# Moving the right-hand SBUF pools of a transformer trunk 32 bytes further in

## The chip, the cores and the metric

The kernel runs on one core of a Trainium2 chip. The metric is the device time of one execution in microseconds. The program before the change took 2705.5, 2704.69 and 2701.03 us in three runs; the median is 2704.69 us. All data is float32, and there is one launch.

## The reference, cut to what matters

Two layers over 1024 tokens of width 1024. The first mixes the tokens with a forgetting attention of 16 heads, the second with a gated MLP whose gate is mixed over blocks of 128 tokens; behind each comes a gated MLP ("FFN") with a short causal convolution.

```
for i in range(2):
    h = modulate(rmsnorm(x, norm1_g[i]), sh1, sc1)
    y = forgetting_attention(h, ...)  if i == 0  else  spatial_gating_mlp(h, ...)
    x = x + g1 * y
    h = modulate(rmsnorm(x, norm2_g[i]), sh2, sc2)
    x = x + g2 * conv_gated_ffn(h, w_up[i], conv_w[i], conv_b[i], w_down[i])
return rmsnorm(x, final_g)
```

The up-projections are `h @ w_up` (1024 x 1024 by 1024 x 5632, twice) and `h @ sgu_w_in` (1024 x 1024 by 1024 x 4096). The vectors `sh`, `sc`, `g` come from six matrix-vector products per layer ("ada") of the conditioning vector `c` after SiLU.

## The kernel before, in words

**Products.** Every float32 product is made of three: each operand is held as a rounded high part and a low rest, and `mm3` (L107) issues high x high, high x low and low x high into one PSUM bank. Each of these is one weight load of the stationary operand (128 x 128) and one matmul that streams the moving operand (mostly 128 x 512).

**Stages.** The attention stage (`fox`) runs to about 827 us of the trace. Then FFN 0, the gated MLP (SGU) and FFN 1 follow. Each of these three has an up part (`up`, L1333) and a down part (`down`, L1468).

**The up part.** A unit is one pair of 128-column slices of the weight. There are 22 units in each FFN and 16 in the SGU. The first two units of a stage are done plainly: eight products of 12 matmuls each (`half1`, `half2`). All later units, 20 + 14 + 20 = 54 of them, are done in seven products (Strassen's scheme in Winograd's form): `p1`, `p5`, `p6`, `p2`, `p7`, `p3`, `p4`, in that order. Each calls `seven` (L1278), which issues 4 x 3 = 12 matmuls into one PSUM bank. The moving operands are seven prepared combinations of the activations, named B11, T1, T2, B21, T3, B22 and T4 in the order of the products; they lie in fourteen tiles `hc0` to `hc13`, two to an operand, and stay for the whole stage. The stationary operands are combinations of the weights, made afresh for every unit in a ring of four tiles `ow0` to `ow3`: a load into `rw` by DMA, sums on VectorE (`sums_u`), and the split into high part (ScalarE, L1131) and low part (VectorE, L1144).

`p1` and `p2` (B11, B21) go to one bank, called `banka` in FFN 0 and FFN 1; `p5` and `p3` (T1, B22) to `bankY`; `p6`, `p7`, `p4` (T2, T3, T4) to `bankX`. After every down part the names `a` and `X` are swapped (L1613), so in the SGU B11 and B21 go to `bankX` and T2, T3, T4 to `banka`.

**The down part.** Both operands of a matmul lie in one `ow` tile: the stationary one in its first half, the moving one in its second.

**Where the tiles lie.** A pool opened without a side grows from the low end of each SBUF partition, a pool with `side="right"` from the high end. The allocator rounds every tile up to 32 bytes. Adding up the tiles in the order of their pools gives their first bytes:

- left: `const`, `small`, `tm`, `x`, `h`, `qkv`, and from the FFN on `hc13` and `hc0` to `hc8`. `hc13` starts at byte 43968, `hc8` at 117696. `x` starts at 11200, and the last `h` tile at 105408. `x`, `h`, `qkv` and these `hc` tiles all start on a multiple of 64.
- right, below byte 229344, which is 32 above a multiple of 64: in the attention `cv`, `raw`, `w` (32 above a multiple of 64), `qq`, `kh`, `kl`, `pt` (a multiple of 64); from the FFN on `hc9` to `hc12` (`hc9` at 135136), `rw`, `ow` (`ow0` at 184288) and `pp0` to `pp2`, all 32 above a multiple of 64.

The parts of a tile that a matmul reads begin at multiples of 512 bytes within these tiles. So with a stationary operand in `ow`, the moving operands B11 and B21 (`hc9` to `hc12`) lie on the same remainder modulo 64 as the weights, and T1, T2, T3, T4 and B22 (`hc13`, `hc0` to `hc8`) lie on another.

**Order of the work.** In the up and down parts TensorE's instructions are chained in program order (`strict`, L103). What TensorE waits for there is an `ow` tile, and so VectorE and ScalarE and, behind them, the DMA into `rw`, all issued on SyncE's queue in program order. `cact` (SiLU of `c`) is read by VectorE in the ada products (L266), and `qg` by ScalarE and VectorE (L695, L697).

Of the kernel before, what the change touches and what calls it, by code (L numbers as in the profile page):

```python
# [8 lines left out]
F32 = mybir.dt.float32  # L9
# [9 lines left out]
P = 128  # L19
S = 1024  # L20
D = 1024
KT = D // P
# [45 lines left out]
class Trunk:  # L68
# [96 lines left out]
    def setup(self):  # L165
        nc, tc, ctx = self.nc, self.tc, self.ctx
        en = ctx.enter_context
        self.const = en(tc.tile_pool(name="const", bufs=1))
        self.small = en(tc.tile_pool(name="small", bufs=3))
        self.tm = en(tc.tile_pool(name="tm", bufs=2))  # L170
        self.xp = en(tc.tile_pool(name="xp", bufs=1, reuse_waits="tile"))
        self.ms = en(tc.tile_pool(name="ms", bufs=2, space=PSUM))
        self.dram = en(tc.tile_pool(name="dram", bufs=1, space=DRAM))
        c = self.const
        self.ident = c.tile([P, P], F32, name="ident")
        make_identity(nc, self.ident)
        self.ones = c.tile([P, P], F32, name="ones")
        nc.vector.memset(self.ones, 1.0)

        self.prm = c.tile([P, 5 * P + 2 * KT], F32, name="prm")  # L180
        self.at = {}
        kp = lambda a: a.rearrange("(k p) -> k p", p=P)
        self.cact = c.tile([P, KT], F32, name="cact")
        first = self.tile(self.tm, [P, 512], F32, "tm")[: 2 * KT, :P]
        o = 5 * P
        for e, nm, src, n in (
            (nc.sync, "c", self.c[0], KT),
            (nc.scalar, "n1_0", self.norm1_g[0], KT),
        ):
            e.dma_start(first[o - 5 * P : o - 5 * P + n], kp(src))  # L190
            self.at[nm] = o
            o += n
        ps = self.tile(self.ms, [P, 512], F32, "ms")
        self.chain("ms", nc.tensor.transpose(ps[:, 0 : 2 * KT], first, self.ident[: 2 * KT, : 2 * KT]))
        nc.vector.tensor_copy(self.prm[:, 5 * P :], ps[:, 0 : 2 * KT])
        self.chain("act", nc.scalar.activation(self.cact, self.col("c", 0, KT), AF.Silu))
        self.mod = {}

        adab = self.tile(self.tm, [P, 512], F32, "tm")[:48, :256]
        self.adabt = c.tile([P, 48, 2], F32, name="adabt")  # L200
        nc.scalar.dma_start(adab, self.ada_b.rearrange("l (r f) -> (l r) f", f=256))
        ps = self.tile(self.ms, [P, 512], F32, "ms")
        for j in range(2):
            i = nc.tensor.transpose(
                ps[:, j * 48 : j * 48 + 48], adab[:, j * P : (j + 1) * P], self.ident[:48, :48]
            )
            if j == 0:
                self.chain("ms", i)
        nc.vector.tensor_copy(self.adabt, ps[:, :96].rearrange("p (j r) -> p r j", j=2))
# [135 lines left out]
    def fox(self):  # L345
        nc, tc = self.nc, self.tc
        w_in, w_out = self.fox_w_in[0], self.fox_w_out[0]
        en = self.ctx.enter_context
# [5 lines left out]
        c = self.const  # L354

        with ExitStack() as es:
# [9 lines left out]
            def T(shape, dt, tag, bufs):  # L366
                return (mp if tag in ("qkv", "fraw") else fp).tile(shape, dt, tag=tag, name=self.name(tag), bufs=bufs)
# [9 lines left out]
            def ps1(nm):  # L377
                return ps_f.tile([P, 512], F32, tag="ps", name=self.name(nm))
# [143 lines left out]
                    o_out(p, half, ps[half])  # L522


            qg = T([P, 1], F32, "qg8", 1)
            nc.vector.tensor_scalar(qg, self.col("qg", 0), DH ** -0.5, None, op0=ALU.mult)
            kg = self.col("kg", 0)
            bf = T([P, H], F32, "bf", 1)
# [509 lines left out]
            for m in range(KT):  # L1038
# [5 lines left out]
                ps = open_ps.get(m) or (banks() if banks else ps1("op"))  # L1044
# [884 lines left out]
```

## Time and profile before

| | |
|---|---|
| median of three runs | 2704.69 us |
| the profiled execution | 2712.99 us |
| its span, first to last instruction | 2711.2 us |
| mean granted TensorE clock | 0.978 |
| TensorE matmuls busy | 2597.6 us, 96% |
| VectorE busy | 2082.7 us, 77% |
| ScalarE busy | 1462.7 us, 54% |
| attention | 0 to 827 us |
| FFN 0: up part, down part | 827 to 1284, 1284 to 1498 us |
| SGU: up part, down part | 1498 to 1870, 1870 to 2030 us |
| FFN 1: up part, down part | 2030 to 2479, 2479 to 2711 us |

The chain of waits is the work that ended last, followed back from the last instruction; a row gives its start and its length in us, the engine, the tile it writes and its line, and how many instructions were merged. A row of the grouped instructions gives the line, engine, operation, tiles (written <- read), shapes and count, then busy us and mean ns of one, then the idle time ahead of it with what ended it. Matmuls overlap, so the mean duration of one is longer than the step from one start to the next; the chain of waits goes by that step.

### The profile page before, as it was taken

To read this page: it belongs to the slowest core of one execution; us is meant where nothing else is said; L and a number is where in the kernel's file an instruction comes from. 1 tells how busy PE (TensorE), PEld (TensorE's weight loads), DVE (VectorE), ACT (ScalarE), POOL (GpSimd) and SP (SyncE) were. 2 spreads that over 40 slices of the span, in tenths; PEclk is the share of its full clock that TensorE was granted. 3 is DMA by queue.
4 is the path that set the end of the run, shared out by engine and by line. 5 is a ranking of instruction groups with operands and counts; after the bars stand their busy time and mean duration, and the time that the engine had idled before them with its cause. 6 is when DMAs were issued, how large, how long until landed. Compare 5 with 4: busy or idle time off the path is not lost.

```text
span 2711.2 us, 35378 instructions
## 1 busy us (share of the span) xinstructions
PE 2597.6 (96%) x12578; PEld 2190.2 (81%) x12578; DVE 2082.7 (77%) x3609; ACT 1462.7 (54%) x2321; POOL 170.4 (6%) x289
## 2 busy tenths in 40 slices
PE   6999999998999999999999999999998999999997
PEld 5988888898777788788888788888876888888886
DVE  7678777888567888888678866765888788877875
ACT  7347666777555445445446544654465545455444
POOL 1122222222200000000000000000000000000000
PEclk9999999998999999999999999999999999999999
DMA  7751111113232344546645346557552343337462
GB/s 230 242 173 53 55 53 53 55 52 109 77 115 70 124 130 135 177 136 204 242 156 172 108 154 185 183 177 271 160 179 73 97 136 115 114 101 280 159 202 90
DMA packets 316521, 379.46 MB, mean 140 GB/s; under 512 B 18872, under 2 KB 196152, under 8 KB 316344
## 3 DMA queue, kind: packets, MB, share of 16 engines
q1 hardware_dynamic: 316120, 377.14, 42.8%
q8 instruction: 99, 1.62, 0.2%
q14 instruction: 78, 0.64, 0.1%
q10 hardware_dynamic: 224, 0.06, 0.0%
HBM read 287.41 MB, written 89.72 MB: 139 GB/s over the span
## 4 chain that ended last, share of the span: by engine, by line
PE 80%; DVE 10%; ACT 4%; DMA 3%; issue 2%; SPq 0%; POOL 0%; DVEq 0%; ACTq 0%; POOLq 0%
PE bankX L104 20%; PE banka L104 18%; PE bankY L104 18%; PE pj L104 7%; PE ms L104 4%; PE o L104 3%; PE s L104 2%; PE ms L157 2%; PE op L104 2%; PE pv L104 2%; DVE ow L1144 1%; DVE hc L1144 1%; PE ms L1753 1%; DVE x L1144 1%; DVE x L1632 1%
## 5 line engine op out<-in xcount | busy, mean ns | idle before, releaser
L1131 ACT CAST ow<-rw 128x1024 fp32r<-128x1024 f32 (+1 forms) x438 | 398.1, 910 | 480.2 <-PE bankY L104 160.8
L1144 DVE TENSOR_TENSOR ow<-rw,ow 128x1024 fp32r<-128x1024 f32 (+1 forms) x438 | 457.6, 1046 | 182.0 <-ACT ow L1131 181.3
L104 PE MATMUL bankX<-hc,ow 128*128 128x512 f32 x1920 | 480.7, 399 | 17.8 <-DVE ow L1144 10.0
L104 PEld LDWEIGHTS bankX<-hc,ow 128*128 128x128 f32 x1920 | 361.5, 190 | 104.4 <-DVE ow L1144 11.9
L104 PE MATMUL banka<-hc,ow 128*128 128x512 f32 x1608 | 396.2, 395 | 1.1 <-DVE ow L1144 1.1
L104 PE MATMUL bankY<-hc,ow 128*128 128x512 f32 x1584 | 396.7, 398 | 0.0
L104 PEld LDWEIGHTS banka<-hc,ow 128*128 128x128 f32 x1608 | 301.4, 189 | 67.7 <-DVE ow L1144 1.4
L104 PEld LDWEIGHTS bankY<-hc,ow 128*128 128x128 f32 x1584 | 296.8, 188 | 70.6 <-issue 1.9
L104 PE MATMUL pj<-x,h 128*128 128x384 f32 (+1 forms) x1536 | 317.3, 349 | 0.2 <-DVE x L119 0.2
L104 PEld LDWEIGHTS pj<-x,h 128*128 128x128 f32 x1536 | 273.1, 194 | 5.0 <-DVE x L119 0.5
L1632 DVE SCALAR_TENSOR_TENSOR x<-x,prm,x 128x1023 f32<-128x1023 f32 (+1 forms) x160 | 204.4, 1279 | 2.7 <-ACT x L1630 2.1
L104 PE MATMUL bankY<-ow 128*128 128x512 f32 x720 | 203.8, 391 | 0.2 <-DVE x L1148 0.2
L104 PE MATMUL banka<-ow 128*128 128x512 f32 x672 | 187.4, 392 | 0.5 <-DVE x L1148 0.5
L104 PEld LDWEIGHTS bankY<-ow 128*128 128x128 f32 x720 | 135.4, 189 | 28.5 <-DVE x L1148 0.6
L104 PE MATMUL bankX<-ow 128*128 128x512 f32 x588 | 156.6, 393 | 0.2 <-DVE ow L1144 0.2
L104 PEld LDWEIGHTS banka<-ow 128*128 128x128 f32 x672 | 125.9, 188 | 27.2 <-ACT x L1181 0.8
L104 PE MATMUL ms<-ow 128*128 128x512 f32 x546 | 140.0, 391 | 0.9 <-DVE pp L1144 0.9
L104 PE MATMUL pv<-pt,w 128*128 128x256 f32 (+1 forms) x640 | 119.1, 296 | 16.2 <-ACT pt L795 13.0
L119 DVE TENSOR_TENSOR pt<-ms,pt 128x512 fp32r<-128x512 f32 (+1 forms) x160 | 100.2, 632 | 41.6 <-ACT pt L795 39.8
L104 PEld LDWEIGHTS bankX<-ow 128*128 128x128 f32 x588 | 110.9, 189 | 24.2 <-issue 0.8
L104 PEld LDWEIGHTS ms<-ow 128*128 128x128 f32 x546 | 102.1, 188 | 23.7 <-DVE pp L1144 2.9
L795 ACT CAST pt<-ms 128x512 fp32r<-128x512 f32 (+1 forms) x160 | 85.2, 539 | 64.7 <-PE ms L157 55.1
(302 smaller groups left out, 3886.2 us busy)
## 6 DMA issues: line engine op xcount, KB each, us to landing
rw<-yd SPq DMA_DIRECT2D x210, 256.0 KB
rw<-in_ffn_w_up_dram SPq DMA_DIRECT2D x88, 512.0 KB
yd<-pp SPq DMA_DIRECT2D x60, 512.0 KB
rw<-in_ada_w_dram SPq DMA_DIRECT2D x48, 512.0 KB
rw<-in_ffn_w_down_dram SPq DMA_DIRECT2D x88, 256.0 KB
rw<-in_sgu_w_in_dram SPq DMA_DIRECT2D x32, 512.0 KB
yd<-x SPq DMA_DIRECT2D x30, 512.0 KB
fraw<-in_fox_w_in_dram SPq DMA_DIRECT2D x96, 128.0 KB
```

Source lines behind the costliest of these rows:

```text
L104: i = self.nc.tensor.matmul(out, lhsT, rhs, start=start, stop=stop, skip_group_check=self.strict)
L119: return (eng or self.nc.vector).tensor_tensor(lo, full, hi.bitcast(F32), op=ALU.subtract)
L157: i = self.nc.tensor.transpose(ps[: s.shape[1], j * P : (j + 1) * P], s, self.ident)
L795: nc.scalar.copy(pt[:, 0, :nb], ps[:, :nb])
L1131: return self.ao(self.nc.scalar.copy(t[:, 0], src))
L1144: return self.vo(self.nc.vector.tensor_tensor(out, a, b, op=op))
L1632: stt(o[:, j:], a[:, : S - j], w[2 - j], o[:, j:], op0=ALU.mult, op1=ALU.add)
L1753: k = nc.tensor.matmul(px[:, b * P : (b + 1) * P], vn[:, b, c * P : (c + 1) * P], sg[:, 0], start=True, stop=True)
```

## The change

A new pool `rim` is opened on the right side, ahead of the other right-hand pools, and `cact` moves into it. It holds 8 float32 numbers per partition, 32 bytes, so all other right-hand tiles come to lie 32 bytes lower. `prm` on the left grows by 8 columns (32 bytes, unused), in the place that `cact` leaves, so all left-hand tiles stay where they are; the copy into `prm` names its columns outright. `qg` takes 9 columns, of which one is used, so its place in the pool grows from 32 to 64 bytes: the tiles of that pool that lie below it (`qq`, `kh`, `kl`, `pt` among them) move by 64 bytes in all and keep their remainder. No instruction is added or taken away.

```diff
+        self.rim = en(tc.tile_pool(name="rim", bufs=1, side="right"))
...
-        self.prm = c.tile([P, 5 * P + 2 * KT], F32, name="prm")
+        self.prm = c.tile([P, 5 * P + 3 * KT], F32, name="prm")
...
-        self.cact = c.tile([P, KT], F32, name="cact")
+        self.cact = self.rim.tile([P, KT], F32, name="cact")
...
-        nc.vector.tensor_copy(self.prm[:, 5 * P :], ps[:, 0 : 2 * KT])
+        nc.vector.tensor_copy(self.prm[:, 5 * P : 5 * P + 2 * KT], ps[:, 0 : 2 * KT])
...
-            qg = T([P, 1], F32, "qg8", 1)
+            qg = T([P, KT + 1], F32, "qg8", 1)[:, :1]
```

## The prediction

> **What bounds the kernel.** I read the page first, then the chain of waits stage by stage, then the groups of instructions.
>
> ```profile
> span 2711.2 us, 35378 instructions
> PE 2597.6 (96%) x12578; PEld 2190.2 (81%) x12578; DVE 2082.7 (77%) x3609; ACT 1462.7 (54%) x2321; POOL 170.4 (6%) x289
> ...
> PE 80%; DVE 10%; ACT 4%; DMA 3%; issue 2%; SPq 0%; POOL 0%; DVEq 0%; ACTq 0%; POOLq 0%
> ```
>
> TensorE is the bound: 80% of the chain that ended last is its own matmuls. So the step from one matmul to the next sets the time. Here is one whole seven-product unit of FFN 0 in the chain, with no other work in between:
>
> ```profile
> 1262.37 2.80 PE bankX L104 x12
> 1265.17 2.72 PE banka L104 x12
> 1267.89 2.80 PE bankY L104 x12
> 1270.70 2.80 PE bankX L104 x12
> 1273.50 2.75 PE banka L104 x12
> 1276.24 2.80 PE bankX L104 x12
> 1279.04 2.80 PE bankY L104 x12
> 1281.84 2.33 PE bankX L104 x10
> ```
>
> Same shapes, same count, no wait, yet two rates. The two banka blocks (B11, B21) take 2.72 and 2.75 us; the five others (T4, T1, T2, T3, B22) take 2.80. The unit takes 1281.84 - 1262.37 = 19.47 us.
>
> Is it the bank? In the SGU the names are swapped, and the fast rate goes with the operand (bankX is now B11 and B21):
>
> ```profile
> 1801.59 2.72 PE bankX L104 x12
> 1804.31 2.80 PE bankY L104 x12
> ...
> 2049.32 2.72 PE banka L104 x12
> 2052.04 2.72 PE bankY L104 x12
> 2054.76 2.80 PE bankX L104 x12
> ```
>
> The last three rows are the plain first units of FFN 1: bankY holds 2.72 while it takes B21, and the next block, the first with T1, is back at 2.80. So neither bank nor scheme decides, but the moving operand's tile.
>
> Two more places tell what about the tile. In the down part both operands lie in one right-hand tile; in the attention's first projections both lie on the left:
>
> ```profile
> 1330.00 0.68 PE banka L104 x3
> ...
> 1344.96 0.68 PE bankX L104 x3
> ...
> 119.98 18.17 PE o L104 x80
> ```
>
> From 1330.00 to 1344.96 there are 22 such rows, 66 matmuls in 14.96 us: 226.7 ns each, or 2.72 us for twelve. On the left it is 18.17/80 = 227.1 ns. The slow blocks take 2.80/12 = 233.3 ns. Right with right (remainders 32 and 32) is fast, left with left (0 and 0) is fast, left with right (0 and 32) is slow.
>
> **The change, part by part.** It adds 32 bytes to the offset between left and right and leaves every left-left and right-right pair as far apart as before, but for the attention's small pool. Exactly the slow blocks are touched. No instruction, wait or DMA is added or moved past a queue.
>
> *The seven-product units.* All 84 matmuls at 226.7 ns make 84 x 0.2267 = 19.04 us instead of 19.47: 0.43 us a unit. With 54 units: 23.2 us. This takes for granted that the 2.75 blocks too come down to 2.72; they start behind a slow block, and the 2.72 blocks of FFN 1 above start behind a fast one.
>
> The Trainium skill speaks against this. "TensorE: Matmul & The Clock Gate", Part 2, first step of the step-by-step, says that TensorE has two independent read ports into SBUF and that loading the next weights takes no bandwidth from the matmul that runs. By that rule it cannot matter where the two operands begin, and the time would stay at 2704.69 us. The trace does not agree: 2.80 against 2.72 us for twelve equal matmuls.
>
> *What of it is not on the chain.* PE's gain counts only where PE sets the end. In FFN 0 the chain leaves it once in mid-stage:
>
> ```profile
> 1087.34 2.80 PE bankX L104 x12
> ...
> 1115.39 6.69 DMA rw<-in_ada_w_dram
> ...
> 1130.51 1.15 DVE ow L1144
> ...
> 1131.70 2.60 PE bankX L104 x10
> ```
>
> From about 1087 to 1131.70, 44 us, it runs over DMAs and VectorE, and what PE gains there is lost: 2.2 units at 20 us, -0.9 us. At the head of each stage the chain runs over VectorE, which makes the seven operands:
>
> ```profile
> 882.00 1.20 DVE hc L1144 x2
> ...
> 888.58 4.63 PE bankX L104 x10
> ...
> 1555.62 1.14 DVE ow L1144
> ...
> 1556.80 2.60 PE banka L104 x10
> ```
>
> The slow blocks of the first two units (8 a stage, 0.08 us each) and some of the third lie ahead of these points. I count them at nothing and take 0.3 us off for the third unit. If all counted it would be +24 x 0.08 = 1.9 us.
>
> *The attention.* There the mixed pairs are `pv` (pt 0, w 32) and the transposes (ident 0; cv, raw, w 32), against equal ones with `x`, `qkv` and `s`:
>
> ```profile
> L104 PE MATMUL pv<-pt,w 128*128 128x256 f32 x512 | 107.8, 306 | 16.2 <-ACT pt L795 13.0 <-DVE pt L119 3.2
> L104 PE MATMUL s<-kh,qq 128*128 128x256 f32 x32 | 9.6, 313 | 0.0
> L157 PE MATMUL ms<-ident,x 128*128 128x128 f32 x152 | 22.4, 272 | 0.0
> L157 PE MATMUL ms<-ident,w 128*128 128x128 f32 x16 | 3.2, 274 | 0.0
> ```
>
> 306 against 313 ns and 274 against 272: no loss to win back, so 0. The bound: 640 `pv` matmuls by the 6.7 ns of the wide ones, 4.3 us.
>
> *VectorE, ScalarE, DMA.* Their operands change remainder too. VectorE's mixed and equal pairs of today cost the same (688 and 691 ns):
>
> ```profile
> L1144 DVE TENSOR_TENSOR rw<-rw,rw 128x512 f32<-128x512 f32 x108 | 74.3, 688 | 1.5
> L1144 DVE TENSOR_TENSOR hc<-hc,rw 128x512 f32<-128x512 f32 x30 | 20.7, 691 | 9.9 <-DMA rw<-in_ffn_w_down_dram 6.6 <-DMA rw<-in_sgu_w_out_dram 3.1
> ```
>
> So 0, and 0 for ScalarE, whose copies read one tile. For landings the trace gives no pair to compare. DMA has 3% of the chain (81 us), and the slow blocks are 3% longer than the fast ones (2.80 to 2.72); 3% of 81 either way is 2.4 us, an estimate for the range. `cact` is read at its new place by the same instructions: 0.
>
> **Sum.** 23.2 - 0.9 - 0.3 = 22.0 us. Against the profiled execution of 2712.99 us (span 2711.2 and 1.8 around it) that gives 2691; it lies 8.3 us above the median of the runs, so against the median 2704.69 - 22.0, rounded to 2682 us.
>
> **The rivals.** *Only a part of it comes (2692 us).* Left-hand moving operands might reach 2.75 us and not 2.72, as blocks do that today follow a slow one. The unit is then 7 x 2.75 = 19.25, 0.22 us less, 12 us in all with the same losses taken in. For it: B11 and B21 stand at 2.75 in nearly every unit. Against: 18.17/80 on the left.
>
> *Left and right differ by themselves (2704 us).* If it is the distance or the side, and not the remainder, a shift of 32 bytes does nothing. The rule of the Trainium skill above ends at the same time. For it: no fast pair in the trace has one operand on each side. Against: `hc8` lies 184288 - 117696 = 66592 bytes below `ow0` and is slow (B22, the row at 1279.04), while `hc9` lies 49152 below it and is fast, in the row at 1265.17 (B11); and left-hand pairs lie up to 94208 bytes apart (`h` to 105408, `x` from 11200) at 227.1 ns. That the change doesn't do what it says, because some tile's size upsets the remainders, ends here too; adding up the sizes, I find none that does.
>
> *Slower: VectorE becomes the bound, and the clock falls.* The place is the up part of the FFNs:
>
> ```profile
> 900.00:1100.00 200.00, 200.00 (x875) 162.23 (x873) 172.01 (x201) 100.66 (x123) 0.00 (x0) 1.00 0.40 129
> ...
> 883.00:894.00 11.00, 6.42 (x15) 4.59 (x16) 10.96 (x12) 2.19 (x4) 0.00 (x0) 0.53 0.23 72
> ...
> 888.58 4.63 PE L104 MATMUL bankX<-hc,ow 128*128 128x512 f32 x10 [4.45 <-DVE ow L1144]
> 893.01 3.22 PE L104 MATMUL banka<-hc,ow 128*128 128x512 f32 x12
> ```
>
> VectorE is busy 172.01 of 200 us (86%). Where PE waited 4.45 us for it, the granted clock over the next 11 us was 0.53, and ten matmuls took 4.63 us instead of 2.27: 2.4 us lost. Nine such stretches eat the gain; from there it is slower, and one in every second unit of the FFNs (20) gives 20 x 2.4 - 22 = +26, 2731 us. Against: a faster unit raises VectorE's share to 86% x 19.47/19.04 = 88%, still short of full, and PE stood still for none of those 200 us.
>
> **How the numbers follow.** The forecast 0.82, the part 0.06, no effect 0.08, slower 0.04. The range runs from all bounds at once (23.2 + 1.9 + 4.3 + 2.4 is 31.8, 2673) to the partial gain (2692); the two other rivals are left out. A time within 0.2% (5.4 us) cannot be told from no change; the first two cases are faster, the third the same.
>
> **What would show it.** In the changed profile the bankX and bankY blocks of twelve in the up parts should stand at 2.72 us like those of the down parts, and the mean of the `hc,ow` groups near that of the `ow` ones:
>
> ```profile
> L104 PE MATMUL bankX<-hc,ow 128*128 128x512 f32 x1920 | 480.7, 399 | 17.8 <-DVE ow L1144 10.0
> ...
> L104 PE MATMUL bankY<-ow 128*128 128x512 f32 x720 | 203.8, 391 | 0.2 <-DVE x L1148 0.2
> ```
>
> FFN 0 should shrink by about 7.7 us, the SGU by 6, FFN 1 by 8.5, the attention and the down parts by nothing. Blocks still at 2.80 would prove the remainder wrong; blocks at 2.72 with longer waits for `ow` would prove that PE was not the bound.

## The result and the profile after

The changed kernel took 2688.12 us (median of five runs) against 2703.49 us of the kernel before in the same series: a ratio of 0.9938 with a 95% interval of 0.9919 to 0.9956, some 17 us less. A second series gave 2685.14 against 2705.7 us, a ratio of 0.992 (0.9907 to 0.9934), some 22 us less. The ratios are taken over all runs of a series; the medians alone are 15.4 and 20.6 us apart. The forecast was 2682 us in a range of 2673 to 2692, 22.0 us less.

The page of the changed kernel (line numbers are two higher below the change):

```profile
span 2686.3 us, 35378 instructions
PE 2573.0 (96%) x12578; PEld 2186.3 (81%) x12578; DVE 2078.6 (77%) x3609; ACT 1463.1 (54%) x2321; POOL 171.5 (6%) x289
...
PE 78%; DVE 11%; ACT 4%; DMA 3%; issue 2%; SPq 1%; POOL 0%; DVEq 0%; ACTq 0%; POOLq 0%
```

TensorE's busy time fell by 2597.6 - 2573.0 = 24.6 us, no other engine's by more than 4.1. The last unit of FFN 0 in the chain of waits of the changed kernel (start, length, what):

```profile
1254.26 2.72 PE banka L104 x12
1256.98 2.72 PE bankY L104 x12
1259.70 2.72 PE bankX L104 x12
1262.42 2.72 PE banka L104 x12
1265.14 2.72 PE bankX L104 x12
1267.86 2.72 PE bankY L104 x12
1270.58 2.72 PE bankX L104 x12
1273.30 0.45 PE ms L104 x2
```

All seven blocks stand at 2.72 us, and the unit takes 1273.30 - 1254.26 = 19.04 us, to the hundredth what the forecast had. At the head of FFN 1, in the same view, the block that was the first slow one now follows at the same step:

```profile
2034.50 2.72 PE bankY L104 x12
2037.22 2.72 PE bankX L104 x12
```

The groups of matmuls (busy us, mean ns of one, idle time ahead) with the moving operand in `hc` come down to those of the down part:

```profile
L104 PE MATMUL bankX<-hc,ow 128*128 128x512 f32 x1920 | 471.3, 394 | 18.5 <-DVE ow L1146 10.3 <-ACT ow L1133 7.8 <-DVE x L1146 0.3
...
L104 PE MATMUL bankY<-hc,ow 128*128 128x512 f32 x1584 | 387.9, 391 | 0.8 <-DVE ow L1146 0.8
...
L104 PE MATMUL bankY<-ow 128*128 128x512 f32 x720 | 203.3, 390 | 0.2 <-DVE x L1150 0.2
```

By stages, from the first `hc` matmul of an up part to its last, in two profiles of each kernel:

| | before | before, again | after | after, again |
|---|---|---|---|---|
| attention and lead-in, us | 827.4 | 819.6 | 823.9 | 825.0 |
| up part of FFN 0 | 456.9 | 456.9 | 449.0 | 449.4 |
| up part of the SGU | 371.5 | 371.6 | 365.9 | 367.2 |
| up part of FFN 1 | 448.7 | 450.0 | 441.3 | 440.0 |
| the three up parts | 1277.0 | 1278.5 | 1256.2 | 1256.6 |
| the profiled execution | 2712.99 | 2707.06 | 2688.12 | 2688.01 |

The up parts lost 20.8 us in the first pair and 22.0 in the second.

### The profile page after: what moved, and what is told of

Same layout as the page of the kernel before. It is cut to its first block, busy times and chain, and to the rows that moved or that the text cites. A ratio compares the mean times of both kernels' runs of the same rounds, so it can differ in the third digit from the quotient of the medians.

```text
span 2686.3 us, 35378 instructions
## 1 busy us (share of the span) xinstructions
PE 2573.0 (96%) x12578; PEld 2186.3 (81%) x12578; DVE 2078.6 (77%) x3609; ACT 1463.1 (54%) x2321; POOL 171.5 (6%) x289
## 3 DMA queue, kind: packets, MB, share of 16 engines
q1 hardware_dynamic: 316120, 377.14, 43.5%
## 4 chain that ended last, share of the span: by engine, by line
PE 78%; DVE 11%; ACT 4%; DMA 3%; issue 2%; SPq 1%; POOL 0%; DVEq 0%; ACTq 0%; POOLq 0%
PE bankX L104 20%; PE banka L104 17%; PE bankY L104 17%; PE pj L104 7%; PE ms L104 5%; PE o L104 3%; PE s L104 2%; PE ms L157 2%; PE op L104 2%; PE pv L104 1%; DVE ow L1146 1%; DVE hc L1146 1%; PE ms L1755 1%; DVE x L1146 1%; DVE x L1634 1%
## 5 line engine op out<-in xcount | busy, mean ns | idle before, releaser
L104 PE MATMUL bankX<-hc,ow 128*128 128x512 f32 x1920 | 471.3, 394 | 18.5 <-DVE ow L1146 10.3
L104 PEld LDWEIGHTS bankX<-hc,ow 128*128 128x128 f32 x1920 | 361.1, 189 | 96.5 <-DVE ow L1146 11.9
L104 PE MATMUL bankY<-hc,ow 128*128 128x512 f32 x1584 | 387.9, 391 | 0.8 <-DVE ow L1146 0.8
```

Source lines behind the costliest of these rows:

```text
L104: i = self.nc.tensor.matmul(out, lhsT, rhs, start=start, stop=stop, skip_group_check=self.strict)
```

## The experiments

In all of them the step of a matmul is the time from its start to the next one's in the trace; means leave out long steps, which hold a wait: those of 285 ns and more, and for the shorter matmuls of the attention's projections (384 and 400 columns) those of 220 ns and more. The distance is that of the stationary operand in `ow` behind the moving one in the left-hand `hc` tiles. It was 140320 bytes before, 32 more than a multiple of 256, and is 140288 after, which is 548 x 256. Two operands whose distance is a multiple of 256 bytes are called in step below, all others out of step; that 256 is the number comes out only at the end.

### Another 32 bytes: 64 in all

```diff
-        self.cact = self.rim.tile([P, KT], F32, name="cact")
+        self.cact = self.rim.tile([P, 2 * KT], F32, name="cact")[:, :KT]
...
-            qg = T([P, KT + 1], F32, "qg8", 1)[:, :1]
+            qg = T([P, 1], F32, "qg8", 1)
```

> The right-hand pools lie 64 bytes further in than before instead of 32, so left and right differ by 32 modulo 64 again. Theory (equal remainder modulo 64 decides): the five left-hand blocks of a unit stand at 2.80 us as before, 19.47 us a unit, the time is that of before, 2703 us. Rival (any shift or the new place helps, or the distance does): blocks at 2.72 us and about 2688 us.

Measured: 2710.91 us, ratio 1.0015 (1.0006 to 1.0025). The chain of waits of this run:

```profile
1230.06 2.80 PE bankX L104 x12
1232.86 2.76 PE banka L104 x12
1235.62 2.80 PE bankX L104 x12
```

The left-hand blocks are back at 2.80 us (233.4 ns a matmul), so it is not the move as such but where it ends. The run is also some 4 us slower than the kernel before, which neither answer had; its up parts took 1279.7 us, 1 to 3 more than before. Much of that lies in the B11 and B21 blocks, which have not moved against their weights: within the seven-product units they step by 230.2 ns here and by 228.8 before, 1.4 ns over some 1380 matmuls, 1.9 us. The rest of the 4 us stays open.

### 96 bytes: equal modulo 64, not modulo 128

```diff
-        self.cact = self.rim.tile([P, KT], F32, name="cact")
+        self.cact = self.rim.tile([P, 3 * KT], F32, name="cact")[:, :KT]
```

> The right-hand pools lie 96 bytes further in than before: left and right agree modulo 64, but differ by 64 modulo 128, while the change as made lets them agree modulo 1024 too. Theory (modulo 64): blocks at 2.72 us as in the change, 2688 us. Rival (the remainder modulo 128 or more decides): blocks at 2.80 us, 2703 us.

Measured: 2698.15 us, ratio 0.9971 (0.996 to 0.9982), between the two answers. So are the blocks:

```profile
1229.22 2.75 PE bankX L104 x12
1231.97 2.77 PE banka L104 x12
1234.74 2.76 PE bankY L104 x12
```

The left-hand matmuls step by 229.9 ns on average, neither 227.3 nor 233.4. Equality modulo 64 brings a part of the gain; my theory as written fell here. The banka row is B11 or B21, in step and still the slowest of the three: these blocks step by 230.1 ns here, against 228.8 in the kernel before, so what runs ahead of them costs them more here.

### Operands 32 bytes apart on one side

The second half of each weight tile is put 32 bytes further back, in the down parts alone; the tiles become 1040 columns wide.

```diff
-        self.owr = Ring([ap.tile([P, 2, S], F32R, name=f"ow{i}") for i in range(4)])
+        self.owr = Ring([ap.tile([P, 2, S + 16], F32R, name=f"ow{i}") for i in range(4)])
...
+        M = slice(512 + 8, S + 8)
...
-                    [(o[:, 0, ms], o[:, 1, ms], o[:, 0, R], o[:, 1, R])],
+                    [(o[:, 0, ms], o[:, 1, ms], o[:, 0, M], o[:, 1, M])],
```

> On top of the change, the second half of each weight tile of the down parts, which holds the moving operand, begins 32 bytes later within the tile. Both operands lie in one right-hand tile, 32 apart modulo 64. Theory (remainder): the 30 x 84 = 2520 matmuls of the down parts, 924 + 672 + 924, go from 226.7 to 233.3 ns, three of them from 0.68 to 0.70 us, in all 2520 x 6.6 ns = 16.6 us, so about 2705 us. Rival (left against right decides, a pair on one side is always fast): 0.68 us, 2688 us.

Measured: 2717.5 us, ratio 1.0037 (1.0023 to 1.0051). In the chain of waits of FFN 0's down part:

```profile
1326.56 0.68 PE bankY L104 x3
1327.24 0.70 PE banka L104 x3
1327.94 0.69 PE bankY L104 x3
```

The rows of the down part stood at 0.68 us before. A pair that lies wholly on the right gets slow as soon as its halves are out of step, so the side is not the cause. But the sizes were off twice. The down parts grew by 3.5 + 3.0 + 3.6 = 10.1 us against the changed kernel and not by 16.6: the low halves lie 4160 bytes behind the high ones, so the three matmuls of a product stand 32, 96 and 224 bytes apart modulo 256 in turn, and step by 230.4 to 231.9 ns. And the up parts, which should not have been touched, lost nearly all of their gain (1276.0 us): the wider tiles put every second one 128 bytes out of step modulo 256, and the low halves 64. That was the first sign that 128 bytes count as well.

### The arena's pool alone, and the attention's pools alone

The first moves only the pool of the FFN and SGU stages, starting from the kernel before; the second starts from the change and moves that pool by 32 bytes more, so that only the attention is left with new remainders. Both add one small memset.

```diff
+        rim = self.ctx.enter_context(self.tc.tile_pool(name="rim", bufs=1, side="right"))
+        self.nc.vector.memset(rim.tile([P, KT], F32, name="rim"), 0.0)
         self.ap = ap = self.ctx.enter_context(
             self.tc.tile_pool(name="arena", bufs=1, side="right", reuse_waits="tile")
```

> Only the right-hand pool of the FFN and SGU stages lies 32 bytes further in; the attention's pools, cact, prm and qg stay where they were. One small memset of the padding tile is added. Theory (only the up parts gain, the attention neither gains nor loses): up parts shorter by 7.8 + 5.6 + 7.4 us as in the change, the time is that of the change, 2688 us, within 3 us. Rival (the attention pays for its new remainders, which is why the timed gain of 15 us is less than the 22 forecast): about 2682 us.

> Only the attention's right-hand pools lie 32 bytes further in, with cact, prm and qg as in the change; the pool of the FFN and SGU stages is moved by another 32 bytes, so its products are mixed as before. One small memset of the padding is added. Theory (the attention neither gains nor loses): up parts as before with blocks at 2.80 us, time that of before, 2706 us within 3. Rival (the attention pays for its new remainders): 3 to 5 us more, about 2710 us.

Measured: the arena alone 2689.11 us, ratio 0.9931 (0.9917 to 0.9945), up parts 1256.7 us; the attention alone 2709.87 us, ratio 1.001 (0.9999 to 1.0021), up parts 1279.2 us. The whole gain comes from the arena (the right-hand pool of the FFN and SGU stages). The attention has no gain. The median of the second run is the rival's figure, and by itself the run does not rule out that the attention pays; but its interval includes no loss at all, its arena lies 64 bytes from its first place as in the first experiment, which was up as much (4.8 and 4.2 us by the medians), and the arena alone, with the attention at its old places, is no faster than the whole change (0.9931 against 0.9938 and 0.992). In the changed kernel the operands of `pv`, 96 apart modulo 256 before, are 128 apart:

```profile
L104 PE MATMUL pv<-pt,w 128*128 128x256 f32 x512 | 108.3, 307 | 15.3 <-ACT pt L797 12.0 <-DVE pt L119 3.3
```

307 ns, where the kernel before had 306.

### Both kernels once more

> The changed kernel once more, on the chip and beside the kernels of this call. Its up parts should again be 20 to 21 us shorter than those of the profile before (1277 us in all); the question is how long its attention stage is this time (823.9 us in the first profile of the change, 827.4 in that of before, 817.9 to 826.3 in four variants). If the attention varies by itself from execution to execution, it lies anywhere in 818 to 828 us; the time is 2688 us within 3.

> The kernel before once more, for a second profile. If the first profile of it (2712.99 us, 7 us above the median of its runs) was a long one, its stages are shorter now, by some 3 us in the attention and some 3 in the up parts, and the up parts come to about 1274 us. If the up parts come to 1277 us again, the gain of the change there is the 20.8 us of the first pair of profiles, and the timed gain of 17 us must be lowered elsewhere.

Measured: the table above and the second series. The attention of the same kernel took 827.4 us in one profile and 819.6 us in another. Over all fourteen profiles it was 815.9 to 819.6 us in the four with a mean granted clock of 0.982, and 822.8 to 827.7 us in the ten with 0.978 to 0.980. In the first 815 us of these traces the granted clock stood at half for 61 to 68 us in the four and for 75 to 85 us in the ten; which of the two brings the other is not shown. So one profile of each kernel cannot tell a few us there, and the first profile of before was a long one in its attention (8 us) but not in its up parts: that half of the expectation missed.

### The projections' weight tiles at 416 and at 448 columns

```diff
-                        t = self.xslot([P, 2, 400], F32R)
+                        t = self.xslot([P, 2, 416], F32R)
```

> On top of the change, the weight tiles of the attention's projections are 416 wide instead of 400, so that their low parts begin 1664 bytes behind the high parts and not 1600: equal modulo 128 instead of 64 apart. One third of the 1344 projections of 384 columns is touched. Theory (the remainder modulo 128 counts, as the shift by 96 bytes showed): the step of the projections falls from 174.6 ns towards 160 + 13.3 = 173.3 ns, 1344 x 1.3 ns = 1.8 us, 2686 us. Rival (with 384 columns the remainder costs nothing): no change against the changed kernel, 2688 us.

> On top of the change, the weight tiles of the attention's projections are 448 wide, so that their low parts begin 1792 bytes behind the high parts: equal modulo 256 to the stationary operand, where 400 gave 64 apart and 416 gave 128 apart. Theory (equality modulo 256 counts, at any width of the moving operand): the step of the 384-column projections falls from 174.6 ns to about 173.3 ns, at most 2 us of the whole, about 2684 us. Rival (384 columns hide it): 174.6 ns and the time of the changed kernel, 2686 us.

Measured: 2685.86 us (ratio 0.9927, 0.9911 to 0.9944) and 2686.57 us (0.9922, 0.9905 to 0.994), beside 0.992 of the changed kernel. The steps were 175.4 and 175.1 ns, against 174.6 and 174.7: no gain at 384 columns, and no better kernel. In the groups of the 448 version:

```profile
L104 PE MATMUL pj<-x,h 128*128 128x384 f32 x1344 | 281.9, 349 | 0.2 <-DVE x L119 0.2
...
L104 PE MATMUL pj<-x,h 128*128 128x400 f32 x192 | 35.4, 343 | 0.0
```

349 ns is what the kernel before had at 384 columns. The second row holds the projections of the first pair of heads, 400 columns wide, and there something changed. In the changed kernel it reads

```profile
L104 PE MATMUL pj<-x,h 128*128 128x400 f32 x192 | 35.8, 346 | 0.0
```

and the step is 182.2 ns there (and 182.2 to 182.3 in the twelve other profiles) and 180.0 with 448. So equality modulo 256 gains at 400 columns too, 2.2 ns of 182 with one matmul in three put in step; over 192 matmuls that is 0.4 us, far below what the times can show. These matmuls run in rows of 30 to 69 without other matmuls between, while those of 384 columns come in rows of at most 23, half of the rows six or shorter; whether that hides the gain at 384 is not shown.

### A sweep of the distance within one tile

On top of the change, a weight tile of the down parts holds stationary high, stationary low, moving high, moving low, and the moving halves begin `off` bytes late, another `off` for each of the seven products of each stage. The puts of one tile become two each.

```diff
+OFF = ((0, 4, 8, 16, 32, 48, 64), (0, 96, 128, 80, 112, 32, 64), (24, 40, 56, 72, 120, 128, 0))
...
-        self.owr = Ring([ap.tile([P, 2, S], F32R, name=f"ow{i}") for i in range(4)])
+        self.owr = Ring([ap.tile([P, 2 * S + 32], F32R, name=f"ow{i}") for i in range(4)])
...
+        def halves(o, p):
+            d = off[p] // 4
+            return [o[:, x : x + S].rearrange("p (a f) -> p a f", a=2) for x in (0, S + d)]
```

> On top of the change, the weight tiles of the down parts are laid out as stationary high, stationary low, moving high, moving low, and the moving halves begin a number of bytes behind equality that differs from product to product: in FFN 0 0, 4, 8, 16, 32, 48, 64 for the products 1, 2, 6, 7, 4, 5, 3 in their order, in the SGU 0, 96, 128, 80, 112, 32, 64, in FFN 1 24, 40, 56, 72, 120, 128, 0. Both operands lie on the right throughout. Theory (the remainder modulo 128 counts): 226.7 ns a matmul at 0 and 128, about 233.4 at 32 and 96, about 229.8 at 64, something between 226.7 and 233.4 at the rest. Rival 1 (modulo 64 alone): 226.7 at 64 too. Rival 2 (only a pair of one tile on each side is ever slow): 226.7 everywhere.

Measured: 2711.98 us in one run, beside 2708.34 of the kernel before in one. The mean steps of the down parts in ns, by how far the moving operand begins behind the stationary one modulo 256 (the other way round than in the up parts):

| bytes apart | 0 | 4 | 8 | 16 | 24 | 32 | 40 | 48 | 56 |
|---|---|---|---|---|---|---|---|---|---|
| step | 228.0 | 238.1 | 233.0 | 230.9 | 233.7 | 233.0 | 232.9 | 232.6 | 232.2 |

| bytes apart | 64 | 72 | 80 | 96 | 112 | 120 | 128 |
|---|---|---|---|---|---|---|---|
| step | 229.6 | 233.6 | 231.5 | 234.2 | 230.3 | 234.7 | 231.7 |

The chain of waits shows the passage from 0 to 4 bytes in FFN 0:

```profile
1307.44 0.68 PE banka L107 x3
1308.12 0.69 PE bankY L107 x3
1308.81 0.71 PE banka L107 x3
1309.53 0.72 PE bankY L107 x3
```

Only 0 is fast, and the cost does not grow evenly with the distance: 64 bytes cost 1.6 ns more than 0, 16 cost 2.9, 96 cost 6.2 and 4 cost 10.1; 128, which the theory and the first rival had as fast, costs 3.7. The up parts of this run told the same: the weight tiles are 8320 bytes apart here, so every second one is 128 off modulo 256, and the steps split into 227.8 to 228.6 ns at 0 and 256 and 232.7 to 232.9 ns at 128 and 384 (modulo 512). So the new theory was equality modulo 256.

### 160 and 288 bytes, arena alone

```diff
-        self.nc.vector.memset(rim.tile([P, KT], F32, name="rim"), 0.0)
+        self.nc.vector.memset(rim.tile([P, 40], F32, name="rim"), 0.0)
```

and with 72 columns in place of 40.

> As the run in which only the FFN and SGU pool is moved, but by 160 bytes instead of 32: left and right agree modulo 64 and 128 but are 128 apart modulo 256. Theory (modulo 256, from the two lots of the sweep that were 128 apart and took 231.7 to 232.9 ns): the left-hand blocks go to about 232.5 ns, 2.79 us for twelve, and nearly all of the gain is lost, about 2703 us. Rival (modulo 64 or 128): 226.7 to 227.3 ns, 2.72 us, 2687 us.

> The same with 288 bytes: left and right agree modulo 256 but are 256 apart modulo 512. Theory (modulo 256): 227 ns, 2.72 us for twelve, 2687 us. Rival (modulo 512 or more): slower blocks, 2692 us or more.

Measured: 160 bytes 2703.34 us, ratio 0.9984 (0.9973 to 0.9994), left-hand steps 232.9 ns; 288 bytes 2683.2 us, ratio 0.991 (0.9892 to 0.9927), 227.3 ns. The chain of waits with 160 bytes:

```profile
1227.38 2.80 PE bankX L104 x12
1230.18 2.73 PE banka L104 x12
1232.92 2.79 PE bankX L104 x12
```

and with 288:

```profile
1227.62 2.72 PE bankX L104 x12
1230.35 2.72 PE banka L104 x12
1233.07 2.72 PE bankY L104 x12
```

With 160 bytes left and right lie on the same remainder modulo 64, and modulo 128, and nearly all of the gain is gone. With 288 they are 256 apart modulo 512, and all of it is there. What counts is the remainder modulo 256, among the distances tried. The mean steps of the left-hand matmuls, over all shifts of the arena:

| shift of the right-hand pool, bytes | 0 | 32 | 64 | 96 | 160 | 288 |
|---|---|---|---|---|---|---|
| distance modulo 256 | 32 | 0 | 224 | 192 | 128 | 0 |
| step, ns | 233.4 | 227.3 | 233.4 | 229.9 | 232.9 | 227.3 |

## Why the prediction was right, and where not

**The bound and the rate.** Right. TensorE set the end in the up parts, and the slow blocks went from 2.80 to 2.72 us. Reading one unit of the chain block by block carried the forecast: 19.04 us was forecast for a unit and 19.04 measured.

**The 2.75 blocks come down too.** Right: banka stands at 2.72 us. B11 and B21 were slowed only by what ran just before them: in the profile before, the first five matmuls of such a block step by 228 to 233 ns and the other seven by about 227.

**What is off the chain.** Right in size. The forecast for FFN 0, the SGU and FFN 1 was 7.7, 6 and 8.5 us; the first pair of profiles gave 7.9, 5.6 and 7.4, the second 7.5, 4.4 and 10.0. The sum of 22.0 lies with 20.8 and 22.0. One term was misread: before the change TensorE holds the chain up to 1098.69 us, so the leave in mid-stage of FFN 0 lasted 33 us and not 44, and the term should have been 0.7 us and not 0.9. The leave is still there after the change, and longer: from 1090.24 us on over a copy, two DMAs and VectorE to 1134.14, 44 us:

```profile
1087.74 2.51 PE bankY L104 x11
...
1093.01 3.17 DMA sgd<-rw
...
1106.97 6.68 DMA rw<-in_ada_w_dram
...
1134.14 3.02 PE bankX L104 x12
```

**The attention, VectorE, ScalarE, DMA at 0.** `pv` stayed at 307 against 306 ns, and the run with the attention alone showed no gain; a loss of up to 0.2% there is not excluded by its interval. VectorE's busy time went from 2082.7 to 2078.6 us and ScalarE's from 1462.7 to 1463.1, and the packets of the DMA queue took 42.8% of the longer span and 43.5% of the shorter, so their new remainders cost nothing that can be seen in the whole. For the transposes the zero rests on less than the forecast took it to: counted modulo 256, `ident` lies 64 bytes from `x` and 96 from `w`, so the two rows it compared (272 and 274 ns) are both out of step. The attention's length varies by itself by 8 us, more than the 4.3 us that the range allowed for it.

**The timed gain.** The first series gave 17 us and the second 22. The profiles of the up parts agree with the second; where the other 5 us of the first went is not shown, but executions of the kernel before differ by up to 14 us (2700.42 to 2714.77 in one series), and its attention alone by 8.

**The step that failed.** Not the size but the rule. The forecast read the remainders 0 and 32 as the cause, modulo 64, from three pairs: right with right, left with left, left with right. All the fast pairs that it showed were equal modulo 256 as well, so it could not tell the two apart, and I did not say so. The runs with 96 and 160 bytes show that equality modulo 64 is not enough: by the forecast's rule they would have gained as much as the change, and they gained some 8 and 4 us. The change hit a multiple of 256 because it took away just the 32 bytes that the layout was off; as far as the rule goes, that was luck.

**The rivals.** Left against right by themselves: out, since 288 bytes are fast and a right-hand pair 32 bytes apart is slow. A part of the gain only: not here, but it is what 96 bytes give. (Its 2692 us should be 2693: 0.22 x 54 is 11.9 us, and half of the losses leaves 11.3.) VectorE as the bound: its share rose from 86% to 88%, as worked out (166.55 of 190 us), without a stall. The row gives the window and its length, the busy us of TensorE, its weight loads, VectorE, ScalarE and GpSimd, then the granted clock, the DMA share and GB/s:

```profile
900.00:1090.00 190.00, 190.00 (x849) 157.57 (x848) 166.55 (x195) 97.20 (x119) 0.00 (x0) 1.00 0.42 133
```

The granted clock of 0.53 that the forecast gives beside a wait is that of 883 to 894 us, so it holds the wait of 4.45 us itself too.

The Trainium skill ("TensorE: Matmul & The Clock Gate", Part 2, step-by-step) says that loading the next weights takes no bandwidth from the running matmul. Read as the forecast read it, that the starts of the two operands cannot matter, it does not agree with these runs: 227 ns with the two operands in step, up to 238.1 ns with them 4 bytes apart. Whether it is the weight load that takes something from the running matmul, the runs do not show.

Not settled: why 256 bytes, what it is in the chip that makes the distance count, and why an offset that is the same for a whole block (32: 233.4 ns) costs more than offsets that change from matmul to matmul (230.4 to 231.9 ns).

## What to carry to other kernels

Where a kernel like this one streams 512 columns of float32 for every weight load, try putting the starts of stationary and moving operands, high and low parts alike, on the same remainder modulo 256 bytes; with the arena alone it cost 32 bytes of padding and gave 2.6% of every matmul that was out of step (6.1 of 233.4 ns). Watch the strides inside tiles and between them as well: widening the weight tiles by 128 bytes undid most of the gain in the up parts, in two runs (1276.0 and 1270.1 us, against 1256 and 1277). Look for it as two rates of the same shape in the chain of waits, and test a suspected modulus by shifts that tell it from its multiples before believing it.

## What the runs showed that was not expected

- The penalty depends on the distance, and not evenly: 227 to 228 ns in step, 229.6 to 229.9 at 64 bytes modulo 256, 231.7 to 232.9 at 128, 233 to 234 at 32 and 96, 238.1 at 4 bytes.
- After a block that is out of step, the first matmuls of a block in step are still slow (2.75 us for twelve instead of 2.72, and up to 2.77 behind blocks of another distance); with equal operands throughout this is gone.
- With moving operands of 256 and 384 columns nothing of it was seen: `pv` stayed at 306 and 307 ns out of step, beside 313 ns of `s` in step, and the projections at 174.7 ns partly out of step and 175.1 ns in step. At 400 columns it was seen: 182.2 ns partly out of step, 180.0 in step.
- Being in step is not all: the matmuls of `s` with 512 columns are in step in both kernels and step by 232 to 234 ns before and by 231 to 232 after. They come in groups of four behind other work; whether that is the slow start of the item above is not shown.
- The same attention stage took 815.9 to 827.7 us, longer where the granted clock of the execution was lower (0.978 against 0.982).
